# Reciprocal sums of attention: repeated along the row by VectorE and turned by two transposes, in place of four products with the identity

## The chip, the core and the metric

The kernel runs on one core of one Trainium2 chip. The metric is the device time of one execution in microseconds. In the profile, PE is TensorE's matrix multiplication and PEld its weight load, DVE is VectorE, ACT is ScalarE, POOL is GpSimd, and SP issues most DMAs.

## What is computed

One inference layer of a decoder with two parallel groups of heads over 1024 prompt tokens and 32 sample tokens (8 sequences of 4 tokens, over a paged cache of 8192 past tokens). Group A is sparse attention: 8 query heads, 2 key/value heads, head dimension 64, over the keys that an indexer selects. Group B is retention. The change lies in group A's attention for the prompt:

```python
logits = jnp.einsum('bqngd,bqknd->bqngk', qg, kg) * (HEAD_DIM ** -0.5)
logits = jnp.where(sel_ok[:, :, None, None, :], logits + bias, -jnp.inf)
probs = jax.nn.softmax(logits, axis=-1)
o = jnp.einsum('bqngk,bqknd->bqngd', probs, vg)
...
ya = jax.nn.silu(ga) * oa.reshape(B, T, D_A)
```

The softmax's division by the row sum, and the gate, are what the changed lines apply to the attention's output.

## The kernel before

The kernel runs input projections, the indexer's scores and selection, retention, attention, and last the output projection with the gated embedding. The order of instructions on each engine is laid out by a planner that works on a simulated timeline from the program's order and its dependences; some places are forced by high priorities and "issue after" marks. The profile shows the order that came out, not the planner's costs.

Attention over the prompt is a loop over 8 blocks of 128 queries (`qb`) and, inside, over the 2 key/value heads (`kv`): sixteen passes, counted 1 to 16 in this text. A pass has n = (qb + 1) * 128 keys and 4 query heads, and does this:

- `near` (L1757, VectorE, 128 x 1024): the relative bias of the last 256 keys plus the mask. The tile has two buffers, so pass k + 2 takes that of pass k.
- For each of the 4 heads (index `i4`), products of queries and keys into a bank `sa` (L1770, L1771, TensorE); VectorE adds `mask` or `near`, writes `L` and keeps the least value `mn` (L1776); ScalarE takes the exponential in place and sums each row into a column of `sm` (L1780). `L` has four buffers for each `kv`, so pass k + 2 writes those of pass k.
- For each block of 128 keys (`kb`), four transposes of the probabilities into a bank `ptp` (L1791, TensorE), a copy to `pT` in SBUF (L1796 on ScalarE, every third, L1794, on VectorE), and products with the values into `ob` (L1799, TensorE). The products for the two head positions `o` each fill 64 of the 128 columns of the array and 64 partitions of the bank.
- The reciprocal `rs` of `sm` (L1802, VectorE), 128 queries by 4 heads. It stands with queries on the partitions, and `ob` has queries along its rows, so the values are turned and repeated: four products with the identity (L1806, TensorE), with one column of `rs` repeated 64 times as the weights, fill `rb`. An fp32 product of this kind is two passes in the profile.
- `gat`, the gate's values for the pass, is multiplied by `rb` (L1809, VectorE), and `ob` by that into `yaT` (L1810, VectorE).

`rb` and `ptp` take turns in the two banks of tag "t". Two generators are worked off in between: `last_norm` (norms of retention, L1733 and L1735) and `sample_attn` (attention of the sample tokens: gathers of cached keys and values by POOL at L1268, transposes `pkg` and `pkw`, products `ls` and `oS`, and VectorE's work around them). A gather waits for the ScalarE instruction that stood latest in the loop when it was issued (L1780 or L1796).

The heads' order in `sm` is column i4 = 2 * o + c2, with o the head's half of the partitions and c2 its half of the columns in `rb`, `ob` and `gat`:

```python
rs = ap_.tile([128, 4], F32, tag="rs", bufs=2, name="rs")
nc.vector.reciprocal(rs, sm)
rb = bank("rb", "t")
for i4 in range(4):
    o, c2 = i4 // 2, i4 % 2
    nc.tensor.matmul(rb[64 * o:64 * o + 64, c2 * 128:c2 * 128 + 128],
                     rs[:, i4:i4 + 1].to_broadcast([128, 64]), ident, start=True, stop=True)
```

## Time and profile before

| what | value |
|---|---|
| median of three runs | 984.95 us (984.34 to 986.95) |
| the profiled execution | 987.33 us |
| its span, first to last instruction | 985.5 us |
| mean granted TensorE clock | 0.983 |
| TensorE busy | 929.4 us (94%) |
| VectorE busy | 643.0 us (65%) |
| ScalarE busy | 447.4 us (45%) |
| `yaT`, first to last of sixteen | 588.9 to 748.4 us |

A matrix product's end is modelled, so a busy TensorE is not TensorE at its peak, and the gaps between its weight loads tell more. A row of the timeline gives the start, the duration, the engine, the line, what is written from what, and in brackets the idle time before it and what ended it; neighbours of one kind are merged and counted.

### The profile page before, as it was taken

The page shows a single profiled execution, that of the slowest core. Times are in us where ns is not written, and L with a number is a line of the kernel's source. Part 1 is how long each engine was busy: PE and PEld are TensorE (multiplying, and loading weights), DVE is VectorE, ACT ScalarE, POOL GpSimd, SP SyncE. Part 2 cuts the span into 40 slices and gives each one's busy share as a digit, 9 for nine tenths or more (in the row PEclk, how much of TensorE's full clock was granted, in tenths as well). Part 3 has the DMA queues.
Part 4 walks back from the last instruction along what each step waited for, and adds up shares of the span by engine and source line. Part 5 has one row for each costly group of instructions (what it writes and reads, how often), then busy time and mean ns, then how long its engine had stood idle before and what let it go on. Part 6 is the DMA issues. An engine that isn't in the chain of part 4 may idle for free.

```text
span 985.5 us, 18931 instructions
## 1 busy us (share of the span) xinstructions
PE 929.4 (94%) x6980; PEld 786.5 (80%) x6980; DVE 643.0 (65%) x1917; ACT 447.4 (45%) x1001; POOL 324.4 (33%) x443
## 2 busy tenths in 40 slices
PE   4999996799998999999999988999999999999998
PEld 3888994467768988899889965666567999899998
DVE  6847668779954769979886467876654224954332
ACT  5645545346232876434333345565555334432210
POOL 4205125113405514516335036554314422133300
PEclk8999999899999999999999969999999999999999
DMA  8313233576544110341225365333222322522211
GB/s 267 119 68 110 102 97 96 199 240 216 173 149 122 44 45 7 82 97 45 61 72 124 102 182 170 108 110 99 60 67 64 107 65 75 165 74 87 93 35 38
DMA packets 102127, 104.36 MB, mean 106 GB/s; under 512 B 22002, under 2 KB 92210, under 8 KB 99602
## 3 DMA queue, kind: packets, MB, share of 16 engines
q1 hardware_dynamic: 96274, 76.93, 26.5%
q0 software_dynamic: 5760, 26.22, 8.7%
q8 instruction: 55, 0.90, 0.4%
q14 instruction: 38, 0.31, 0.1%
HBM read 80.36 MB, written 22.76 MB: 105 GB/s over the span
## 4 chain that ended last, share of the span: by engine, by line
PE 75%; DMA 9%; DVE 7%; issue 3%; ACT 2%; POOL 2%; SPq 2%; ACTq 0%; DVEq 0%; POOLq 0%
PE pb L277 5%; PE pb L278 4%; PE pb L279 4%; PE ob L1799 4%; PE ptp L1791 4%; PE pg L287 3%; PE pg L289 3%; PE pg L288 3%; PE po L287 3%; PE po L289 3%; PE po L288 3%; PE pvg L287 2%; PE pvg L288 2%; PE pvg L289 2%; PE pqk L287 2%
## 5 line engine op out<-in xcount | busy, mean ns | idle before, releaser
L1268 POOL DMA_INDIRECT kvs<-in_cache_kv,idx x64 | 63.3, 989 | 85.4 <-ACT pT L1796 33.8
L287 PE MATMUL pqk<-whi_qkb,xh 128*128 128x256 f32 x256 | 73.4, 287 | 2.7 <-DVE rp L1109 1.2
L287 PE MATMUL pvg<-whi_vgb,xh 128*128 128x256 f32 x256 | 75.1, 293 | 0.6 <-DVE rp L1109 0.6
L288 PE MATMUL pvg<-wlo_vgb,xh 128*128 128x256 f32 x256 | 73.7, 288 | 0.8 <-POOL wlo_vgb L197 0.8
L287 PE MATMUL po<-whi_o,yTh 128*128 128x256 f32 x256 | 73.3, 286 | 0.4 <-DVE yaT L1810 0.4
L288 PE MATMUL pqk<-wlo_qkb,xh 128*128 128x256 f32 x256 | 73.5, 287 | 0.0
L289 PE MATMUL pvg<-whi_vgb,xl 128*128 128x256 f32 x256 | 73.3, 286 | 0.0
L289 PE MATMUL po<-whi_o,yTl 128*128 128x256 f32 x256 | 72.9, 285 | 0.0
L289 PE MATMUL pqk<-whi_qkb,xl 128*128 128x256 f32 x256 | 72.8, 284 | 0.0
L287 PE MATMUL pg<-whi_g,yTh 128*128 128x256 f32 x256 | 72.7, 284 | 0.0
L288 PE MATMUL po<-wlo_o,yTh 128*128 128x256 f32 x256 | 72.6, 284 | 0.0
L289 PE MATMUL pg<-whi_g,yTl 128*128 128x256 f32 x256 | 72.3, 283 | 0.0
L288 PE MATMUL pg<-wlo_g,yTh 128*128 128x256 f32 x256 | 72.2, 282 | 0.0
L197 POOL TENSOR_TENSOR wlo_g<-wraw_g,whi_g 128x256 fp32r<-128x256 f32 x32 | 27.2, 881 | 88.1 <-ACT whi_g L196 88.0
L1780 ACT ACTIVATE L<-L,mn 128x128 f32<-128x128 f32 (+7 forms) x64 | 49.6, 777 | 13.2 <-DVE mn L1776 10.7
L1988 DVE TENSOR_TENSOR sgm<-pu,sgm 128x256 f32<-128x256 f32 x32 | 13.6, 424 | 64.2 <-PE pu L289 60.7
L545 DVE SCALAR_TENSOR_TENSOR score<-r,wi,score 128x384 f32<-128x384 f32 (+5 forms) x42 | 43.0, 1023 | 18.8 <-ACT r L544 16.7
L287 PEld LDWEIGHTS pqk<-whi_qkb,xh 128*128 128x128 f32 x256 | 48.3, 188 | 4.3 <-issue 2.3
L287 PEld LDWEIGHTS po<-whi_o,yTh 128*128 128x128 f32 x256 | 49.0, 191 | 2.2 <-issue 1.6
L287 PEld LDWEIGHTS pvg<-whi_vgb,xh 128*128 128x128 f32 x256 | 48.4, 189 | 2.7 <-PE pvg L296 0.8
L287 PEld LDWEIGHTS pg<-whi_g,yTh 128*128 128x128 f32 x256 | 48.8, 190 | 1.6 <-issue 1.2
L544 ACT ACTIVATE r<-si 128x384 f32<-128x384 f32 (+5 forms) x48 | 35.8, 758 | 30.2 <-PE si L386 20.7
(540 smaller groups left out, 3067.8 us busy)
## 6 DMA issues: line engine op xcount, KB each, us to landing
wraw_qkb<-in_w_in SPq DMA_DIRECT2D x16, 256.0 KB
wraw_vgb<-in_w_in SPq DMA_DIRECT2D x16, 256.0 KB
wraw_o<-in_w_out SPq DMA_DIRECT2D x8, 512.0 KB
qas<-qas_d SPq DMA_DIRECT2D x8, 512.0 KB
xr<-in_x_prompt SPq DMA_DIRECT2D x8, 512.0 KB
wraw_g<-in_w_ple_gate SPq DMA_DIRECT2D x8, 512.0 KB
out_y_prompt<-sgm SPq DMA_DIRECT2D x32, 128.0 KB
qas_d<-qst SPq DMA_DIRECT2D x8, 384.0 KB
```

Of the source, the lines that this page charges most:

```text
L277: nc.tensor.matmul(pt[:m, :n], wh, xh[:, k, ts], start=(k == 0), stop=False)
L278: nc.tensor.matmul(pt[:m, :n], wh, xl[:, k, ts], start=False, stop=False)
L279: nc.tensor.matmul(pt[:m, :n], wl, xh[:, k, ts], start=False, stop=(k == KC - 1))
L287: nc.tensor.matmul(pt[:, :n], ah, hi[:, k, :n], start=(k == 0), stop=False)
L288: nc.tensor.matmul(pt[:, :n], ah, lo[:, k, :n], start=False, stop=False)
L289: nc.tensor.matmul(pt[:, :n], al, hi[:, k, :n], start=False, stop=(k == kc - 1))
L544: nc.scalar.activation(r[:, :n], s[:, :n], AF.Relu)
L545: nc.vector.scalar_tensor_tensor(sc, r[:, :n], wi[:, qb, h:h + 1], sc if h else place[:, :n], op0=ALU.mult, op1=ALU.add)
L1268: return nc.gpsimd.indirect_dma_start(out=dst, out_offset=None, in_=kvflat, in_offset=bass.IndirectOffsetOnAxis(ap=idx, axis=0))
L1780: behind[0] = nc.scalar.activation(L[:, :n], L[:, :n], AF.Exp, bias=least, scale=-1.0, accum_out=sm[:, i4:i4 + 1])
L1791: nc.tensor.transpose(tp[:, i4 * 128:i4 * 128 + 128], P[i4][:, kb * 128:kb * 128 + 128], ident)
L1799: nc.tensor.matmul(ob[64 * o:64 * o + 64, :256], vtok[:, kb, kv * 64:kv * 64 + 64], pT[:, o * 256:o * 256 + 256], start=(kb == 0), stop=(k ...
```

## The change

The tile `rs` is gone; its name now stands for the first quarter of this pass's `near` (128 x 256), which has been read by then. VectorE's reciprocal reads each of the four values 64 times and writes 256, ordered so that a transpose of 128 columns puts each head's value on the 64 partitions of its half. Two full transposes on TensorE fill `rb`. What follows, `gat` and `yaT`, is as it was.

```diff
-            rs = ap_.tile([128, 4], F32, tag="rs", bufs=2, name="rs")
-            nc.vector.reciprocal(rs, sm)
+            rs = near[:, 0].rearrange("p (c x) -> p c x", c=2)
+            nc.vector.reciprocal(rs.rearrange("p c (o d) -> p c o d", o=2),
+                                 sm.rearrange("p (o c) -> p c o", o=2)[:, :, :, None].to_broadcast([128, 2, 2, 64]))
             rb = bank("rb", "t")
-            for i4 in range(4):
-                o, c2 = i4 // 2, i4 % 2
-                nc.tensor.matmul(rb[64 * o:64 * o + 64, c2 * 128:c2 * 128 + 128],
-                                 rs[:, i4:i4 + 1].to_broadcast([128, 64]), ident, start=True, stop=True)
+            for c2 in range(2):
+                nc.tensor.transpose(rb[:, c2 * 128:c2 * 128 + 128], rs[:, c2], ident)
```

Of the kernel before, what the change touches and what calls it, by code (L numbers as in the profile page):

```python
# [11 lines left out]
F32 = mybir.dt.float32  # L12
# [119 lines left out]
def tile_step(ctx: ExitStack, tc: tile.TileContext, I, O):  # L132
    nc = tc.nc

    def pool(name, bufs=1, **kw):
        return tc.tile_pool(name=name, bufs=bufs, reuse_waits="tile", **kw)
# [18 lines left out]
    def bank(name, tag="b"):  # L155
        if tag in kept.get("tags", ()):
            return kept["pool"].tile([128, 512], F32, tag="s", bufs=1, name=name)
        return psum["pool"].tile([128, 512], F32, tag=tag, bufs=psum["bufs"][tag], name=name)
# [6 lines left out]
    def C(name, rows=128):  # L165
        o, w = _CW[name]
        return cst[:rows, o:o + w]

    ident = C("ident")
# [342 lines left out]
    with pool("ix", side="right") as ix:  # L512
# [125 lines left out]
        def more():  # L638
            pace[0] += 0.3
            while pace[0] >= 1:  # L640
                pace[0] -= 1
                next(last, None)
# [178 lines left out]
    def step(gen, n=1):  # L821
        for _ in range(n):
            next(gen, None)
# [301 lines left out]
    def chunk_mm(qk, vv, tb, rows, mask_ap, hp):  # L1125

        r = bank("ret", "c")
        nc.tensor.transpose(r[:, 0:rows], qk[:rows, 0:128], ident[:rows, :rows])
        nc.tensor.transpose(r[:, 128:128 + rows], qk[:rows, 128:256], ident[:rows, :rows])
        qkT = rt.tile([128, 256], F32, tag="qkT", bufs=2, name="qkT")  # L1130
        rv = r[:, :256].rearrange("p (a r) -> p a r", a=2)[:, :, :rows]
        qv = qkT.rearrange("p (a r) -> p a r", a=2)[:, :, :rows]
        nc.scalar.copy(qv, rv)
        e = second[:, (tb % 4) * 128:(tb % 4) * 128 + 128]
        sm = rt.tile([128, 2, 128], F32, tag="sm", bufs=2, name="sm")
        for j, sc in enumerate((r[:rows, 256:256 + rows], e[:rows, :rows])):
            js = slice(j * 64, j * 64 + 64)
            nc.tensor.matmul(sc, qkT[js, 128:128 + rows], qkT[js, 0:rows], start=True, stop=True)
            nc.vector.tensor_tensor(sm[:rows, j, :rows], sc, mask_ap, op=ALU.mult)
        return r, qkT, sm  # L1140
# [452 lines left out]
    for hp in range(4):  # L1593
# [27 lines left out]
        for tb in range(8):  # L1621
# [8 lines left out]
            r, qkT, sm = chunk_mm(qk, vv, tb, 128, tri, hp)  # L1630
            o = r[:, 0:128]
# [10 lines left out]
            for j in range(2):  # L1642
                nc.tensor.matmul(o[:, j * 64:j * 64 + 64], sm[:, j, :], vv[:, j * 64:j * 64 + 64],
                                 start=(tb == 0 and j == 0), stop=(j == 1))
# [46 lines left out]
    ap_ = as_.enter_context(pool("att", side="right"))  # L1691
# [6 lines left out]
    def load_q(qb):  # L1698
        q = ap_.tile([128, 8, 128], F32R, tag="qas", bufs=2, name=f"qas{qb}")
        last_q[0] = nc.sync.dma_start(q.bitcast(F32), qas_d[:, :, qb * 128:(qb + 1) * 128]).ins  # L1700
        return q
# [41 lines left out]
    for qb in range(8):  # L1743
        qas = qnext
        if qb < 7:
            qnext = load_q(qb + 1)
            if qb == 3:
                with tc.issue_after(last_q[0]):
                    nc.sync.dma_start(gpost, I["g_post"].to_broadcast([128, D]))
        n = (qb + 1) * 128  # L1750
        w = min(n, 256)
        gat = ap_.tile([128, 4, 128], F32, tag="gat", bufs=2, name="gat")
        nc.sync.dma_start(gat, ga_d[:, :, qb * 128:n])
        mn_src = caus[:, 256 - w:] if qb < 2 else mask[:, OFF[qb] + n - w:OFF[qb] + n]
        for kv in range(2):
            near = ap_.tile([128, 4, 256], F32, tag="near", bufs=2, name="near")
            nc.vector.tensor_tensor(near[:, :, 256 - w:], toep[:, 4 * kv:4 * kv + 4, 256 - w:],  # L1757
                                    mn_src[:, None, :].to_broadcast([128, 4, w]), op=ALU.add)
            sm = ap_.tile([128, 4], F32, tag="sm", bufs=2, name="sm")
            P = []  # L1760
            for i4 in range(4):
                h = 4 * kv + 2 * (i4 % 2) + i4 // 2
                L = (atl, at)[kv].tile([128, T], F32, tag="L", bufs=4, name="L")
                P.append(L)
                mn = ap_.tile([128, 4], F32, tag="mn", bufs=4, name="mn")
                least, i = 3.0e38, 0
                for c in range(0, n, 512):
                    wc = min(512, n - c)
                    s = bank("sa")
                    nc.tensor.matmul(s[:, :wc], qas[:, h, :], kah[kv][:, c:c + wc], start=True, stop=False)  # L1770
                    nc.tensor.matmul(s[:, :wc], qas[:, h, :], kal[kv][:, c:c + wc], start=False, stop=True)  # L1771
                    cut = min(max(n - w, c), c + wc)
                    for x0, x1, add in ((c, cut, mask[:, OFF.get(qb, 0) + c:OFF.get(qb, 0) + cut]),
                                        (cut, c + wc, near[:, h - 4 * kv, cut - n + 256:c + wc - n + 256])):
                        if x1 > x0:
                            latest[0] = nc.vector.tensor_tensor_reduce(  # L1776
                                L[:, x0:x1], s[:, x0 - c:x1 - c], add, 1.0, least,
                                op0=ALU.add, op1=ALU.min, accum_out=mn[:, i:i + 1]).ins
                            least, i = mn[:, i:i + 1], i + 1
                behind[0] = nc.scalar.activation(L[:, :n], L[:, :n], AF.Exp, bias=least, scale=-1.0,  # L1780
                                                 accum_out=sm[:, i4:i4 + 1])
                more(0.4 + n / 1200)
            if qb > 1:
                step(ln)
            ob = bank("ob", "o")
            for kb in range(qb + 1):
                if kb == 1 and qb > 1:
                    step(ln)
                tp = bank("ptp", "t")
                for i4 in range(4):  # L1790
                    nc.tensor.transpose(tp[:, i4 * 128:i4 * 128 + 128], P[i4][:, kb * 128:kb * 128 + 128], ident)  # L1791
                pT = ap_.tile([128, 512], F32, tag="pT", bufs=4, name="pT")
                if kb % 3 == 2:
                    nc.vector.tensor_copy(pT, tp)  # L1794
                else:
                    behind[0] = nc.scalar.copy(pT, tp)  # L1796
                more(0.65)
                for o in range(2):
                    nc.tensor.matmul(ob[64 * o:64 * o + 64, :256], vtok[:, kb, kv * 64:kv * 64 + 64],  # L1799
                                     pT[:, o * 256:o * 256 + 256], start=(kb == 0), stop=(kb == qb))  # L1800
            rs = ap_.tile([128, 4], F32, tag="rs", bufs=2, name="rs")
            nc.vector.reciprocal(rs, sm)  # L1802
            rb = bank("rb", "t")
            for i4 in range(4):
                o, c2 = i4 // 2, i4 % 2
                nc.tensor.matmul(rb[64 * o:64 * o + 64, c2 * 128:c2 * 128 + 128],  # L1806
                                 rs[:, i4:i4 + 1].to_broadcast([128, 64]), ident, start=True, stop=True)
            gv = gat[:, 2 * kv:2 * kv + 2, :]
            nc.vector.tensor_tensor(gv, rb[:, :256].rearrange("p (c q) -> p c q", c=2), gv, op=ALU.mult)  # L1809
            nc.vector.tensor_tensor(yaT[:, 2 * kv:2 * kv + 2, qb * 128:n],  # L1810
                                    ob[:, :256].rearrange("p (c q) -> p c q", c=2), gv, op=ALU.mult)
            if qb > 1:
                step(ln)
# [219 lines left out]
```

## The prediction

> **What bounds the kernel now.** I read the page's totals first, then the stage of the change (attention, 580 to 750 us of the span) by engine, then the chain that ended last inside it, and last the single rows around the changed lines.
>
> The page, part 1:
>
> ```profile
> PE 929.4 (94%) x6980; PEld 786.5 (80%) x6980; DVE 643.0 (65%) x1917; ACT 447.4 (45%) x1001; POOL 324.4 (33%) x443
> ```
>
> The stage in four stretches:
>
> ```profile
> core 0: us, PE busy (x) PEld busy (x) DVE busy (x) ACT busy (x) POOL busy (x), PEclk, DMA share, GB/s
> 580.00:600.00 20.00, 16.91 (x100) 11.74 (x101) 14.80 (x60) 12.45 (x41) 10.70 (x10) 0.75 0.39 108
> 600.00:640.00 40.00, 37.73 (x296) 24.48 (x294) 34.16 (x137) 22.84 (x59) 22.51 (x24) 1.00 0.51 146
> 640.00:720.00 80.00, 80.00 (x599) 50.18 (x595) 56.10 (x199) 44.28 (x90) 35.41 (x37) 1.00 0.32 89
> 720.00:750.00 30.00, 28.92 (x239) 18.11 (x237) 13.68 (x48) 15.24 (x30) 4.04 (x4) 1.00 0.13 41
> ```
>
> The chain that ended last, cut to 580 to 750 us (437 pieces; its shares by line and its longest piece):
>
> ```profile
> by line: PE ob L1799 23.4%; PE ptp L1791 22.6%; PE sa L1770 11.8%; PE sa L1771 10.0%; PE oS L1533 4.9%; PE ls L1499 4.9%; PE rb L1806 4.4%; PE pkg L1485 3.9%; issue 2.4%; DMA kvs<-in_cache_kv,idx 2.1%; ACT L L1780 1.8%; ACT pT L1796 1.3%; P
> 599.15 3.55 DMA kvs<-in_cache_kv,idx
> ```
>
> TensorE holds the chain almost throughout, and the products with the identity (rb, L1806) are 4.4% of these 170 us, 7.5 us, or 0.47 us each. So work taken off TensorE here counts. But VectorE is not idle company: it is busy 74% of the first 20 us, 85% of the next 40, 70% of the next 80. There is one large hole on TensorE, 3.55 us at 599 us for a gather.
>
> **VectorE: one value becomes 256.** Before, the reciprocal takes 4 values per partition; after, the same 4 are read 64 times each and 256 quotients are written. The kernel has no reciprocal of that width, so its price comes from the narrow ones (three groups by line with their shapes, and the answers for three single lines, with least/median/greatest ns and first and last start):
>
> ```profile
> L1802 DVE RECIPROCAL rs<-sm x16: 158/172/180, 584.6 to 728.4; 128x4 f32<-128x4 f32 x16
> L260 DVE RECIPROCAL ry_x<-ry_x 128x1 f32<-128x1 f32 x8 | 1.2, 154 | 0.3 <-ACT ry_x L259 0.3
> L731 DVE RECIPROCAL wd<-wd 128x6 f32<-128x6 f32 x6 | 1.1, 182 | 0.2
> L1158 DVE RECIPROCAL gy<-gy 128x16 f32<-128x16 f32 x3 | 0.7, 235 | 0.0
> L1201 DVE RECIPROCAL wi<-wi x1: 266/266/266, 580.0 to 580.0; 128x18 f32<-128x18 f32 x1
> L1757 DVE TENSOR_TENSOR near<-toep,mask x12: 1205/1219/1361, 592.7 to 695.6; 128x1024 f32<-128x1024 f32 x12
> L1757 DVE TENSOR_TENSOR near<-toep,cst x4: 684/958/1225, 570.6 to 585.8; 128x512 f32<-128x512 f32 x2, 128x1024 f32<-128x1024 f32 x2
> ```
>
> From 4 to 16 values the time goes from 172 to 235 ns: 5.25 ns a value. From 1 to 6 it is (182 - 154)/5 = 5.6, from 4 to 18 it is (266 - 172)/14 = 6.7. Ordinary work is far cheaper: from 512 to 1024 elements L1757 goes from 684 to 1219 ns, 1.04 ns an element. So a reciprocal is not a streaming operation here, and 252 further values cost 252 x 5.25 = 1.32 us; the new instruction takes about 1.5 us. Bounds: 252 x 1.04 = 0.26 us more if wide ones stream, 252 x 6.7 = 1.69 us more by the steepest pair. I take 1.32, since all pairs of reciprocals lie at 5 to 7. Sixteen of them: +21.1 us (bounds 4.2 and 27.0).
>
> [...]
>
> What of the 21.1 us lies on the path? The reciprocals start at 584.6 to 728.4 us: four in the first stretch, five in the second, six in the third, one in the last. In 580 to 640 us VectorE is idle for 60 - 48.96 = 11.04 us, and nine reciprocals add 9 x 1.32 = 11.9: even if every gap could be used it does not fit. The gaps are waits for products of other engines, so I take half of them as usable: 11.9 - 5.5 = 6.4 us on the path (bounds: 0.9 with all usable, 11.9 with none). In 640 to 720 us 23.9 us idle stand against 6 x 1.32 = 7.9; I take 0.2 us for each, a late copy of pT (every third is VectorE's) or a late L: 1.2 us (bounds 0 and 7.9). The last one at 728 us has free time behind it: 0, its cover being TensorE's work until the end of attention; without it 1.3. Together +7.6.
>
> **TensorE: eight passes become two.** The rows of its weight loads at three places, in order of time, show what a change of column width costs, which no group shows:
>
> ```profile
> 590.27 0.19 PEld L1771 LDWEIGHTS sa<-kalo,qas 128*128 128x128 f32 x1
> 590.59 0.42 PEld L1806 LDWEIGHTS rb<-cst,rs 128*64 128x64 f32 x8
> 591.19 0.19 PEld L1770 LDWEIGHTS sa<-kahi,qas 128*128 128x128 f32 x1 [0.17 <-issue]
> ...
> 672.76 0.20 PEld L1799 LDWEIGHTS ob<-pT,vtok 128*64 128x64 f32 x4 [0.37 <-issue]
> 673.34 0.42 PEld L1791 LDWEIGHTS ptp<-cst,L 128*128 128x128 f32 x4 [0.39 <-issue]
> 673.93 0.20 PEld L1799 LDWEIGHTS ob<-pT,vtok 128*64 128x64 f32 x4 [0.17 <-issue]
> 674.20 0.63 PEld L1806 LDWEIGHTS rb<-cst,rs 128*64 128x64 f32 x8
> 675.00 0.42 PEld L1485 LDWEIGHTS pkg<-cst,kvs 128*128 128x128 f32 x4 [0.17 <-issue]
> ...
> 718.05 0.20 PEld L1799 LDWEIGHTS ob<-pT,vtok 128*64 128x64 f32 x4
> 718.32 0.63 PEld L1806 LDWEIGHTS rb<-cst,rs 128*64 128x64 f32 x8
> 718.87 0.30 PEld L1799 LDWEIGHTS ob<-pT,vtok 128*64 128x64 f32 x4
> ...
> 721.36 0.87 PEld L1791 LDWEIGHTS ptp<-cst,L 128*128 128x128 f32 x8
> ```
>
> Eight transposes load in 0.87 us, four in 0.42: 0.11 us each, so two add 0.22. Going from 64 columns (128*64, ob and rb) to 128 leaves the loader idle 0.39 us "for nothing the profile shows", going back 0.17. The old products stand in ob's width, the new transposes in ptp's. I count the sixteen places as they stand now:
> - three between full-width products (as at 590.59): rb takes 591.19 - 590.59 = 0.60, two transposes 0.22; saves 0.38 x 3 = 1.14.
> - seven behind ob and ahead of full width (as at 674.20): from ob to the next full-width load 675.00 - 673.93 = 1.07; without rb it is 673.34 - 672.76 = 0.58, with two transposes 0.80; saves 0.27 x 7 = 1.89.
> - four between two ob (as at 718.32): now 718.87 - 718.05 = 0.82; from ob over four transposes to ob it is 673.93 - 672.76 = 1.17, over two 0.95; loses 0.13 x 4 = 0.52.
> - two between ob and 32-column products; about 0.1 each saved by the same differences, 0.2.
>
> That is 2.7 us saved. If all sixteen fell beside full-width work it would be 16 x 0.38 = 6.1; if all fell between two ob, a loss of 2.1. I take 2.7, since the order around them is not the change's. In all 128 passes become 32 (two for a product, as x8 for four shows; one for a transpose, as x4 for a bank of ptp shows), and their issue is inside these differences.
>
> [...]
>
> **The tile rs becomes the first quarter of near.** Nothing is saved or spent on memory that shows, but near has two buffers, so the one for the pass after next may now be written only when this pass's transposes have read it; before, it waited only for the L that add it. Two passes early and two late, VectorE's and TensorE's rows (near of passes 3 and 16; the reciprocal of pass 14 and rb of passes 1 and 14), and what frees L in pass 14 (released by the ptp just ahead of rb of pass 12):
>
> ```profile
> 582.69 1.23 DVE L1757 TENSOR_TENSOR near<-toep,cst 128x1024 f32<-128x1024 f32 x1
> 585.90 1.13 PE L1806 MATMUL rb<-cst,rs 128*64 128x128 f32 x8
> ...
> 695.57 1.23 DVE L1757 TENSOR_TENSOR near<-toep,mask 128x1024 f32<-128x1024 f32 x1
> 696.74 0.18 DVE L1802 RECIPROCAL rs<-sm 128x4 f32<-128x4 f32 x1
> 718.54 0.66 PE L1806 MATMUL rb<-cst,rs 128*64 128x128 f32 x8
> ...
> 686.22 0.69 DVE L1776 CUSTOM_DVE_ANT_0 L<-sa,mask 128x512 f32<-128x512 f32 x1 [2.51 <-PE ptp L1791]
> 686.71 0.63 PEld L1806 LDWEIGHTS rb<-cst,rs 128*64 128x64 f32 x8
> ```
>
> Near runs 3 us (early) to 23 us (late) ahead of the transposes that it will have to wait for, in all fourteen cases. So it will move, from VectorE's free time to just behind rb. Its reader hardly comes earlier: the four L of a pass are freed by the last ptp of the pass two before, half a us ahead of rb there. In late passes the mask part of L comes first and covers the wait; behind near in VectorE's queue stand then the copies of pT and the L parts, for which ACT's exponentials wait. In passes 3 and 4 near is needed at once; the hole of 3.55 us for the gather stands behind them as cover, and without it they cost 2 x 1.22 us. Bounds: 0, and 14 x 1.22 = 17.1 us if all came on the path. I take 0, as the free place is half a us from where L starts anyway.
>
> DMAs, ScalarE's work, SP's queue and POOL's gathers do not change in number. The gathers wait for ACT's copies of pT, so they shift with them.
>
> **Sum.** +7.6 (VectorE) - 2.7 (TensorE) + 0 (near) = +4.9 us. The profiled execution took 987.33 us with a span of 985.5, 2.4 above the median of the three runs: 992.2 by it, 989.9 by the median 984.95. I say 990.
>
> **Rivals.**
> - VectorE's extra is hidden (faster). If the planner puts each reciprocal where VectorE waits anyway, or wide reciprocals stream (0.26 us), only TensorE's saving is left: 2.7 to 6.1 us, 979 to 982. For it: between 640 and 720 us nearly three times the idle time that is needed, and products that come 21.8 us after their reciprocal in pass 14 (696.74 and 718.54). Against: 11.9 us into 11.0 in 580 to 640. It decides once less than 2.7 us of the 21.1 stay on the path.
> - The two cancel: 2 to 5 us of VectorE on the path, 985 plus or minus 3.
> - Near's wait is the bound: the fourteen come on the path with 17.1 us, less 2.7: +14.4, 999. For it: near moves in every pass, and 600 to 640 us has VectorE at 85%. Against: L is freed next to it.
> - VectorE's value costs more than the slope that I took: at 6.7 ns nine instructions add 15.2 us in 580 to 640, 9.7 of it beyond half the gaps, with 1.2 and -2.7: +8.2, 993; with every extra on the path (27.0 - 2.7) 1009. [...]
>
> **How the numbers follow.** Forecast (+3 to +9, 988 to 994): 0.42. Hidden: 0.18. Cancelled: 0.22. Near: 0.08. Dearer value or more of it on the path: 0.10. A measurement of this kernel tells about 0.3%, 3 us, from no change. Faster 0.18, same 0.24 (0.22 and the forecast's lower edge), slower 0.58. The range leaves out the best case's end and the worst: 981 to 1001.
>
> **What would show it.** The stage is read from the first to the last yaT:
>
> ```profile
> L1810 DVE TENSOR_TENSOR yaT<-ob,gat x16: 394/420/426, 588.9 to 748.4; 128x256 f32<-128x256 f32 x16
> ```
>
> Its length, 588.9 to 748.4 us, should grow by about 5 us, and the rest stay unchanged. Further: the reciprocal at L1801 to L1803 at 1.3 to 1.8 us x16 and VectorE's total up by about 21 us; rb with 32 instead of 128 passes; near starting after the transposes of the pass two before, with an idle ahead of it or moved in order; VectorE above 90% in the 60 us from the start of attention. Wrong if the reciprocal streams, if the chain of the stage is as solid on TensorE as before, or if the order of work changes elsewhere.

## The result

| kernel | median | runs | ratio, 95% interval |
|---|---|---|---|
| before | 984.64 us | 4 (983.35 to 986.95) | |
| after | 998.03 us | 4 (995.92 to 998.7) | 1.0128 (1.0102 to 1.0155) |

The change costs 1.28%, 12.6 us. The direction is as forecast, the size is not: +5 was said, and the value lies in the upper part of the range. The profiled execution of the changed kernel took 998.04 us, 10.7 more than that of before. Later comparisons are each made against runs of the kernel before on the same chip, whose median went from 984.5 to 989.6 us with the chip; so the ratios are what to compare.

The changed kernel's page, its totals, and the four stretches of the stage, as shown for the kernel before:

```profile
PE 934.3 (94%) x6884; PEld 786.6 (79%) x6884; DVE 665.1 (67%) x1917; ACT 449.3 (45%) x1001; POOL 323.5 (32%) x443
```

```profile
580.00:600.00 20.00, 15.63 (x72) 11.28 (x72) 15.18 (x50) 10.85 (x37) 9.13 (x8) 0.59 0.32 94
600.00:640.00 40.00, 34.29 (x236) 21.01 (x233) 34.95 (x116) 20.46 (x54) 18.91 (x20) 0.96 0.46 137
640.00:720.00 80.00, 75.68 (x536) 47.38 (x535) 66.02 (x204) 43.34 (x91) 33.60 (x37) 0.98 0.31 87
720.00:750.00 30.00, 29.70 (x206) 17.67 (x203) 21.05 (x62) 18.60 (x34) 7.86 (x9) 1.00 0.23 68
```

VectorE's total rises by 22.1 us, TensorE executes 96 passes fewer. Yet TensorE is less busy in the first three stretches, with holes that it did not have, while VectorE goes from 70 to 83% in the third. The chain that ended last in the stage (580 to 750 us), and the one wait of TensorE that grew most, of before and after (580 to 745 us; total us, times, longest):

```profile
by line: PE ob L1799 17.3%; PE ptp L1791 16.5%; DMA kvs<-in_cache_kv,idx 11.0%; PE sa L1770 8.6%; PE sa L1771 6.9%; issue 4.7%; PE ls L1499 4.2%; DVE L L1776 4.2%; PE oS L1533 3.3%; ACT L L1780 3.2%; PE pkg L1485 2.7%; ACT pT L1796 1.6%; PE
```

```profile
PEld pkg L1485 <- DMA kvs<-in_cache_kv,idx: 1.2, 1, 1.2
```

```profile
PEld pkg L1485 <- DMA kvs<-in_cache_kv,idx: 8.0, 7, 1.9
```

The gathers of cached keys hold 11% of the chain, 2.1% before. That looks like a cause; an experiment below takes this wait away, and the loss stays. The changed instructions:

```profile
L1802 DVE RECIPROCAL near<-sm x16: 1730/1746/1753, 585.0 to 743.9; 128x256 f32<-128x256 f32 x16
L1806 PEld LDWEIGHTS rb<-cst,near x32: 137/142/230, 586.8 to 758.4; 128*128 128x128 f32 x32
L1757 DVE TENSOR_TENSOR near<-toep,mask x12: 1162/1212/1218, 601.1 to 731.6; 128x1024 f32<-128x1024 f32 x12
L1809 DVE TENSOR_TENSOR yaT<-ob,gat x16: 358/416/425, 590.7 to 759.7; 128x256 f32<-128x256 f32 x16
```

The reciprocal takes 1.746 us, sixteen of them 25.2 us more than before. The last near starts at 731.6 us, before at 695.6: it has moved behind the transposes. From the first to the last yaT it is 169.0 us, before 159.5. How one reciprocal stands in VectorE's queue, in the timeline (the transposes of pass 10, then near and the L of pass 12, with pass 11's reciprocal among them):

```profile
675.20 0.20 PEld L1806 LDWEIGHTS rb<-cst,near 128*128 128x128 f32 x2 [0.38 <-issue]
...
676.02 1.22 DVE L1757 TENSOR_TENSOR near<-toep,mask 128x1024 f32<-128x1024 f32 x1
676.06 0.28 PE L1771 MATMUL sa<-kalo,qas 128*128 128x256 f32 x1
...
677.76 0.69 DVE L1776 CUSTOM_DVE_ANT_0 L<-sa,mask 128x512 f32<-128x512 f32 x1
678.38 1.75 DVE L1802 RECIPROCAL near<-sm 128x256 f32<-128x256 f32 x1
...
678.70 0.28 PE L1771 MATMUL sa<-kalo,qas 128*128 128x256 f32 x1
...
680.32 0.47 DVE L1776 CUSTOM_DVE_ANT_0 L<-sa,near,mn 128x256 f32<-128x256 f32 x1
...
680.40 0.14 PEld L1485 LDWEIGHTS pkg<-cst,kvs 128*128 128x128 f32 x1 [1.39 <-DMA kvs<-in_cache_kv,idx]
...
680.72 0.48 DVE L1776 CUSTOM_DVE_ANT_0 L<-sa,near,mn 128x256 f32<-128x256 f32 x1
```

The two L with near, at 680.32 and 680.72, read banks that the products at 676.06 and 678.70 had filled, at 676.34 and 678.98; both stood behind the reciprocal in VectorE's order. Meanwhile TensorE, in its own order, stood 1.39 us at keys that had not landed.

### The profile page after: what moved, and what is told of

It reads as the page before. It is cut to its first block, busy times and chain, and to the rows that moved or that the text cites. A ratio compares the mean times of both kernels' runs of the same rounds, so it can differ in the third digit from the quotient of the medians.

```text
span 996.2 us, 18764 instructions
## 1 busy us (share of the span) xinstructions
PE 934.3 (94%) x6884; PEld 786.6 (79%) x6884; DVE 665.1 (67%) x1917; ACT 449.3 (45%) x1001; POOL 323.5 (32%) x443
## 4 chain that ended last, share of the span: by engine, by line
PE 71%; DVE 10%; DMA 9%; issue 4%; ACT 3%; POOL 2%; SPq 1%; DVEq 0%; ACTq 0%; POOLq 0%
PE pb L277 5%; PE pb L278 4%; PE pb L279 4%; PE ob L1799 3%; PE pg L287 3%; PE ptp L1791 3%; PE pg L289 3%; PE pg L288 3%; PE po L287 3%; PE po L288 3%; PE po L289 3%; PE pvg L287 2%; PE pvg L288 2%; PE pvg L289 2%; PE pox L879 2%
## 5 line engine op out<-in xcount | busy, mean ns | idle before, releaser
L1268 POOL DMA_INDIRECT kvs<-in_cache_kv,idx x64 | 65.4, 1022 | 97.0 <-ACT pT L1796 38.3
L1780 ACT ACTIVATE L<-L,mn 128x128 f32<-128x128 f32 (+7 forms) x64 | 49.4, 774 | 12.8 <-DVE mn L1776 12.5
L1791 PE MATMUL ptp<-cst,L 128*128 128x128 f32 x288 | 50.9, 295 | 1.7 <-ACT L L1780 1.2
L1791 PEld LDWEIGHTS ptp<-cst,L 128*128 128x128 f32 x288 | 32.8, 145 | 24.1 <-issue 18.3
```

The source lines that it names most:

```text
L1268: return nc.gpsimd.indirect_dma_start(out=dst, out_offset=None, in_=kvflat, in_offset=bass.IndirectOffsetOnAxis(ap=idx, axis=0))
L1780: behind[0] = nc.scalar.activation(L[:, :n], L[:, :n], AF.Exp, bias=least, scale=-1.0, accum_out=sm[:, i4:i4 + 1])
L1791: nc.tensor.transpose(tp[:, i4 * 128:i4 * 128 + 128], P[i4][:, kb * 128:kb * 128 + 128], ident)
```

## The experiments

Four theories were tested. V: the long reciprocal's time on VectorE is the loss. N: near's wait for the transposes is. P: any edit makes the planner lay out another order, and the loss is a draw of that. G: the loss goes by way of the gathers.

| kernel | ratio to before, 95% | at 985 us |
|---|---|---|
| changed | 1.0128 (1.0102 to 1.0155) | +12.6 |
| changed, storage of its own for the 256 values | 1.0129 (1.0090 to 1.0167) | +12.7 |
| long reciprocal alone, products as before | 1.0153 (1.0123 to 1.0182) | +15.1 |
| half as long, products as before | 1.0055 (1.0032 to 1.0079) | +5.4 |
| long one added, read by nobody | 1.0117 (1.0088 to 1.0145) | +11.5 |
| short reciprocal, VectorE copy, near waits | 1.0045 (1.0019 to 1.0071) | +4.4 |
| the same, near free | 0.9988 (0.9964 to 1.0011) | -1.2 |
| near's wait alone, first runs | 1.0043 (1.0017 to 1.0070) | +4.2 |
| near's wait alone, second runs | 1.0029 (1.0014 to 1.0045) | +2.9 |
| changed, reciprocal in four pieces, near free | 1.0085 (1.0056 to 1.0114) | +8.4 |
| changed, reciprocal held back | 1.0148 (1.0111 to 1.0184) | +14.6 |

**Storage of its own.** The 256 values go to two stretches of the constants that the attention no longer needs.

```diff
-            rs = near[:, 0].rearrange("p (c x) -> p c x", c=2)
+            rs = C(("cos", "sin")[kv])[:, :256].rearrange("p (c x) -> p c x", c=2)
```

> The whole change, but the 256 repeated reciprocals lie in storage of their own (a stretch of the constants that is no longer read), so near is free as early as before. Theory V (VectorE's longer reciprocal, 1.75 us in place of 0.17, is the loss): 994 to 999 us, as the changed kernel. Theory N (near, taken up two passes on, waits for the transposes): back to 982 to 987. Theory P (the planner lays out another order, in which TensorE meets cached keys that have not landed; each edit gives a draw of its own): anywhere from 984 to 999, and the more idle time of TensorE ends with the gathered keys, the slower.

+1.29%, the changed kernel's loss. Taking near's wait away brings nothing back; N falls as the cause of this loss.

**The long reciprocal alone.** As above, and the products with the identity as before.

```diff
-            for c2 in range(2):
-                nc.tensor.transpose(rb[:, c2 * 128:c2 * 128 + 128], rs[:, c2], ident)
+            for i4 in range(4):
+                o, c2 = i4 // 2, i4 % 2
+                nc.tensor.matmul(rb[64 * o:64 * o + 64, c2 * 128:c2 * 128 + 128],
+                                 rs[:, c2, 64 * o:64 * o + 64], ident, start=True, stop=True)
```

> VectorE's part alone: 256 repeated reciprocals in storage of their own, and the four products with the identity as before (their weights are 64 repeated columns instead of one column read 64 times). V: 996 to 1001, the changed kernel without TensorE's saving of about 3 us. N: 984 to 988. P: anywhere from 985 to 1000.

+1.53%: V holds. With the run above, on the same chip, it also prices TensorE's part: 1000.08 with products, 996.83 with transposes, 3.2 us less, though the two intervals overlap.

**Half the length.** Before with 128 values, each of the four 32 times.

```diff
-            rs = ap_.tile([128, 4], F32, tag="rs", bufs=2, name="rs")
-            nc.vector.reciprocal(rs, sm)
+            rs = C(("cos", "sin")[kv])[:, :128].rearrange("p (c o d) -> p c o d", c=2, o=2)
+            nc.vector.reciprocal(rs, sm.rearrange("p (o c) -> p c o", o=2)[:, :, :, None].to_broadcast([128, 2, 2, 32]))
...
-                                 rs[:, i4:i4 + 1].to_broadcast([128, 64]), ident, start=True, stop=True)
+                                 rs[:, c2, o, 0:1].to_broadcast([128, 64]), ident, start=True, stop=True)
```

> The kernel before with a reciprocal of 128 values (each of the 4 repeated 32 times) in storage of its own; the four products read one column each as before. At the 6.25 ns a value that the changed kernel shows it should take 0.95 us, 0.78 more than before, 12.4 us in sixteen passes: half of what the 256 values add. If each added us of VectorE costs its share (proportional): +7.5 us, 992. If the free time of VectorE takes up the first half and only the rest costs: +2 to +4, 986 to 989. If any other laying-out of the order costs alike, whatever VectorE's load: +12 to +15.

+5.4 us for 12.4 us of VectorE, between the two forecasts: the first half costs 0.44 of its time, and from here to the long one (+9.7 for 12.8 us) 0.76. The interval, 3.2 to 7.8 us, holds the proportional +7.5 too, so that the second half costs more is not shown. The price of a value, from the groups by line of this kernel, of the long one alone and of the pieces below:

```profile
L1802 DVE RECIPROCAL cst<-sm 128x128 f32<-128x128 f32 x16 | 15.1, 946 | 1.6 <-ACT L L1780 1.6
```

```profile
L1802 DVE RECIPROCAL cst<-sm 128x256 f32<-128x256 f32 x16 | 27.9, 1744 | 2.9 <-ACT L L1780 2.9
```

```profile
L1784 DVE RECIPROCAL cst<-sm 128x64 f32<-128x64 f32 x64 | 34.7, 544 | 5.6 <-ACT L L1780 4.8 <-issue 0.8
```

From 64 to 128 values 6.28 ns each, from 128 to 256 6.23.

**A load without a consumer.** Before, with a long reciprocal behind the short one, written where nobody reads it.

```diff
             nc.vector.reciprocal(rs, sm)
+            nc.vector.reciprocal(C(("cos", "sin")[kv])[:, :256].rearrange("p (a d) -> p a d", a=4),
+                                 sm[:, :, None].to_broadcast([128, 4, 64]))
```

> The kernel before, with a reciprocal of 256 values added behind the narrow one, whose result nobody reads: VectorE's time alone, 16 x 1.75 = 28 us, with no consumer. If the loss is VectorE's occupation (other work stands behind the long instruction): +13 to +18, 998 to 1003 beside 985. If the loss is that the products or transposes wait for a longer reciprocal: within 3 us of before.

+1.17%, a little below what V expected: it is VectorE's occupation that costs, not a product that waits longer for its reciprocal.

**A short reciprocal and a copy**, once into near (near waits), once into storage of its own.

```diff
+            r4 = ap_.tile([128, 4], F32, tag="rs", bufs=2, name="rs")
+            nc.vector.reciprocal(r4, sm)
             rs = near[:, 0].rearrange("p (c x) -> p c x", c=2)
-            nc.vector.reciprocal(rs.rearrange("p c (o d) -> p c o d", o=2),
-                                 sm.rearrange("p (o c) -> p c o", o=2)[:, :, :, None].to_broadcast([128, 2, 2, 64]))
+            nc.vector.tensor_copy(rs.rearrange("p c (o d) -> p c o d", o=2),
+                                  r4.rearrange("p (o c) -> p c o", o=2)[:, :, :, None].to_broadcast([128, 2, 2, 64]))
```

> The change with a narrow reciprocal (4 values) and a VectorE copy that repeats them into near's first quarter; transposes and near's wait stay. The copy should take 0.3 to 0.45 us, so VectorE is relieved of some 18 us of the added 25. V: 984 to 988. N: 995 to 999, as the changed kernel. P: anywhere from 984 to 999.

> Narrow reciprocal (4 values), a VectorE copy of 0.29 us that repeats them into storage of their own, two transposes: no longer reciprocal, and near does not wait. If near's wait is worth the 4 us that the run with this wait alone showed: 983 to 986. If the 4.4 us of the run with copy and near came from the copy's 4.6 us on VectorE instead: 988 to 990. With nothing but TensorE's saving: 982.

+0.45% with near's wait, -0.12% without: repeating by a copy takes back all that the long reciprocal costs, and then near's wait shows, some 0.57% (5.6 us) between the two. The copy, in the second kernel:

```profile
L1804 DVE COPY cst<-rs x16: 278/291/480, 592.6 to 739.2; 128x256 f32<-128x256 f32 x16
```

0.29 us for what costs 1.57 us by reciprocals. The two transposes' saving is not to be told from nothing here (interval 0.9964 to 1.0011).

**Near's wait alone**, in the kernel before; run twice.

```diff
-            rs = ap_.tile([128, 4], F32, tag="rs", bufs=2, name="rs")
+            rs = near[:, 0, :4]
             nc.vector.reciprocal(rs, sm)
```

> The kernel before with only one thing changed: the 4 reciprocals are written into near's first four columns, and the four products read them there, so near waits as in the changed kernel. V: 984 to 986. N: 994 to 999. P: not the same as before although nothing was added, 982 to 996.

> The kernel before with near's wait alone, once more and in more rounds: its first runs gave +0.43% but the one profile put less than 1 us into attention, its start having been 7 us late. If near's wait costs time by itself: +4 to +6, with attention longer by as much in the profile. If the first result was the scatter of what comes ahead of attention: within 2 us of before.

+0.43% and +0.29%, so by itself it does cost 3 to 4 us. First near, fourth and last yaT of the first kernel's execution, then of the second's, and the fourth yaT of before:

```profile
577.64 1.29 DVE L1757 TENSOR_TENSOR near<-toep,cst 128x512 f32<-128x512 f32 x2 [0.76 <-DMA toep<-toep_d]
...
610.55 0.42 DVE L1810 TENSOR_TENSOR yaT<-ob,gat 128x256 f32<-128x256 f32 x1
...
756.12 0.42 DVE L1810 TENSOR_TENSOR yaT<-ob,gat 128x256 f32<-128x256 f32 x1 [2.62 <-PE ob L1799]
```

```profile
L1757 DVE TENSOR_TENSOR near<-toep,cst x4: 684/954/1218, 573.7 to 594.8; 128x512 f32<-128x512 f32 x2, 128x1024 f32<-128x1024 f32 x2
...
610.34 0.42 DVE L1810 TENSOR_TENSOR yaT<-ob,gat 128x256 f32<-128x256 f32 x1
...
756.24 0.42 DVE L1810 TENSOR_TENSOR yaT<-ob,gat 128x256 f32<-128x256 f32 x1 [2.61 <-PE ob L1799]
```

```profile
607.36 0.42 DVE L1810 TENSOR_TENSOR yaT<-ob,gat 128x256 f32<-128x256 f32 x1
```

Attention starts 3.9 us apart and ends 0.1 us apart; before it starts at 570.6. So these two executions of one kernel reached attention 3.9 us apart, and at the fourth yaT 0.2 us of that is left. Behind the fourth pass the two agree: 145.6 and 145.9 us to the last yaT, where before takes 141.0 and the three kernels with a copy and near free 139.8 to 141.0. So the wait's cost lies there in both traces; with a copy and near's wait it is less clear (141.9).

**Without the gathers' wait**, in both kernels.

```diff
-                    if behind[0] is not None:
-                        tc.add_manual_dep(got.ins, behind[0].ins.name, mybir.DependencyInfo(
-                            mybir.DependencyClass.Sync, mybir.DependencyReason.DATA))
```

> The changed kernel, but the gathers of cached keys and values no longer wait for ScalarE's latest exponential or copy (a pacing wait; what they need of data and buffers they still wait for). Theory G (VectorE's longer reciprocal makes ScalarE's pieces later, the gathers wait for these, and TensorE, in order, stands at the transposes of keys that have not landed): most of the loss goes by this wait, so this kernel against the same edit of the kernel before is at most 5 us slower, and TensorE's idle time ended by gathered keys falls from 8 us to about 1. Theory V (VectorE's throughput itself is the bound): still 10 to 14 us slower than the same edit of the kernel before.

> The kernel before without the gathers' wait for ScalarE: the control of the run above. The gathers start earlier and meet other transfers; 980 to 992, by itself nothing that tells the theories apart.

1049.55 and 1036.86 us, 1.0611 and 1.0473 times before. The difference stays at 12.7 us, as V said, and in neither trace does TensorE wait for gathered keys any more. But with both kernels some 50 us slower this alone does not decide.

**Nobody waits for the gathered keys**, in both kernels (toep is noted in keys where it is made). The sample tokens' attention reads toep in place of what was gathered.

```diff
-            kw = kws[p % 2]
-            kv = [kvs[(2 * p + j) % 4] for j in range(2)]
+            kw = keys[0][:, :2]
+            kv = [keys[0], keys[0]]
```

> The kernel before, but the sample tokens' attention reads its cached keys and values from the table of biases, which lies in SBUF and has the shape, instead of from what was gathered; the gathers run as before and nobody waits for them (this leaves the sample outputs' use of the cache out). Control of the next run. TensorE stood 1.2 us at gathered keys before, so 982 to 986.

> The changed kernel with the same edit: TensorE never waits for gathered keys. Theory G (the longer reciprocal costs time by way of the gathers: ScalarE's pieces late, gathers late, TensorE in order stands at keys that have not landed, 8 us in the changed kernel's profile): the difference to the control falls from 12.6 to 5 us or less. Theory V (VectorE's throughput and the queue behind each reciprocal): still 10 to 13 us over the control, with the idle time now ended by ScalarE's copies, L and banks.

985.80 and 999.13 us: 13.3 us apart by the medians, 15.3 by the two ratios (1.0122 / 0.9968 = 1.0155). G falls. Who waits instead, in the waits of the first and the second (580 to 760 us):

```profile
ACT L L1781 <- DVE mn L1777: 13.1, 15, 3.0
```

```profile
ACT L L1781 <- DVE mn L1777: 33.0, 20, 3.8
```

ScalarE's exponentials stand 20 us longer for VectorE's least values. The same wait in before and in the changed kernel themselves:

```profile
ACT L L1780 <- DVE mn L1776: 10.7, 14, 1.8
```

```profile
ACT L L1780 <- DVE mn L1776: 12.5, 19, 2.0
```

There it hardly grows, and TensorE's wait for keys grows by 6.8 us. That this is the same lateness, seen where TensorE's next instruction happened to be the gathers', is a reading and not shown. In the six other kernels with more values to take, those on the gathers aside, the wait is 15.6 to 22.0 us; in the eight executions with the short reciprocal alone it is 9.0 to 14.7 (580 to 765 us).

**In four pieces.** 64 values behind each head's exponential, in storage of their own.

```diff
+                o, c2 = i4 // 2, i4 % 2
+                rs = C(("cos", "sin")[kv])[:, :256].rearrange("p (c x) -> p c x", c=2)
+                nc.vector.reciprocal(rs[:, c2, 64 * o:64 * o + 64], sm[:, i4:i4 + 1].to_broadcast([128, 64]))
```

> The change with the reciprocals split: 64 values behind each head's exponential, into storage of their own, four instructions of about 0.55 us in place of one of 1.75 us; 2.2 us a pass, so 7 us more of VectorE in all. Throughput (VectorE's sum in the stage counts): +15 to +20 over before. Blocking (L, mn and copies stand behind one long instruction, short ones let them through): +3 to +9.

+0.85% with 34.7 us of reciprocals in place of 27.9 (the rows above). By VectorE's sum alone it should be slower than the undivided one. It is rather faster, but the intervals (0.56 to 1.14 and 0.90 to 1.67%) overlap: short blocks may soften it, and that is not settled.

**Held back** until the pass's last copy of pT (turned_ names it) has been issued.

```diff
+            with tc.issue_after(turned_.ins):
+                nc.vector.reciprocal(rs.rearrange("p c (o d) -> p c o d", o=2),
```

> The changed kernel with the long reciprocal held back until the pass's last copy of the turned probabilities has been issued, in place of as soon as the sums are there. Throughput: +11 to +14, as the changed kernel. Blocking of the L parts and exponentials two passes on: +4 to +8, as it then stands where a pass ends. If its product is then waited for by TensorE: over +14.

+1.48% (1.11 to 1.84%), more than the +4 to +8 us of blocking: another place does not help. Between the other two forecasts it does not decide.

**The copy on other engines**, with a short reciprocal and near free.

> Narrow reciprocal, the repeating copy by ScalarE into storage of its own, two transposes. VectorE's work is that of the kernel before, TensorE saves about 2.5 us, ScalarE (55% busy in the stage) gets 16 copies of about 0.35 us: 980 to 985 if ScalarE's copies are hidden, 985 to 989 if they delay exponentials and copies.

> The same with GpSimd making the repeating copy, about 1 us each behind the gathers in its queue, which wait for ScalarE: 981 to 985 if the products come late enough, 986 to 995 if the copies stand behind waiting gathers and the banks of the transposes are held.

1.0006 (0.9985 to 1.0026) with ScalarE's copy, 1.0000 (0.9981 to 1.0019) with GpSimd's; the copies take 0.40 us on each, where about 1 us was expected of GpSimd:

```profile
L1804 ACT COPY cst<-rs x16: 387/404/428, 588.0 to 730.4; 128x256 f32<-128x256 f32 x16
```

```profile
L1804 POOL COPY cst<-rs x16: 396/403/1114, 584.4 to 727.4; 128x256 f32<-128x256 f32 x16
```

Neither beats the kernel before. P is not borne out as the cause: the kernels with 256 reciprocals a pass lose 0.85 to 1.53%, the three with a copy and near free lie within 0.12% of before, although each has an order of its own. The profiled executions say the same, from the first near to the last yaT: 177.8 us before, 176.7 to 179.4 in those three, 184.2 with 128 values, 185.8 to 194.4 in the six with 256.

## Why the prediction was wrong in size

- **A value's price.** The slope taken from 4 to 18 values was right in kind, and the rival of a streaming reciprocal is gone. Its size was low: 5.25 ns was said, 6.2 to 6.3 are measured, close to the steepest pair of rows (6.7). That is 25.2 us in place of 21.1. With the share unchanged it makes 9.1 us on the path and a sum of +6.4: the price alone explains 1.5 us of the miss.
- **The share on the path: this step failed.** 7.6 of 21.1 us were put on the path, 0.36; the long reciprocal alone shows 15.1 of 25.2, 0.60, the load without a consumer 11.5 of 27.5, 0.42 (their intervals overlap). Within it the stretch from 640 us was taken for nearly free, 1.2 us. The eighth and the last yaT of before, of the changed kernel, and of the long reciprocal alone:

```profile
640.39 0.42 DVE L1810 TENSOR_TENSOR yaT<-ob,gat 128x256 f32<-128x256 f32 x1 [0.19 <-PE ob L1799]
...
748.37 0.42 DVE L1810 TENSOR_TENSOR yaT<-ob,gat 128x256 f32<-128x256 f32 x1 [2.61 <-PE ob L1799]
```

```profile
648.87 0.42 DVE L1809 TENSOR_TENSOR yaT<-ob,gat 128x256 f32<-128x256 f32 x1
...
759.69 0.42 DVE L1809 TENSOR_TENSOR yaT<-ob,gat 128x256 f32<-128x256 f32 x1 [0.46 <-PE oT L1539]
```

```profile
644.10 0.42 DVE L1811 TENSOR_TENSOR yaT<-ob,gat 128x256 f32<-128x256 f32 x1
...
757.36 0.42 DVE L1811 TENSOR_TENSOR yaT<-ob,gat 128x256 f32<-128x256 f32 x1
```

  The changed kernel is 8.5 us late by pass 8, 1.0 of it from ahead of the first near; 6.4 was said for about this part. By the last pass it is 11.3 late, 2.8 more in spite of TensorE's saving. The long reciprocal alone is 3.7 and then 9.0 late: 5.3 us more where 1.2 was said. From pass 8 to the last it is 108.0 us before and 106.6 to 109.9 in the three kernels with a copy and near free, 110.8 in the changed kernel, 113.3 to 114.4 with the long reciprocal alone, with storage of its own and with the load. These are single executions; that of the long reciprocal alone was the fastest of its four.

  The idle VectorE was taken for room, and the trace of before did have room: behind the reciprocals of passes 13 and 14 VectorE stood idle for 2.51 us (the prediction shows the row at 686.22) and 2.13 us. Before, and the same two passes in the changed kernel:

```profile
683.55 0.16 DVE L1802 RECIPROCAL rs<-sm 128x4 f32<-128x4 f32 x1
...
699.05 0.58 DVE L1505 CUSTOM_DVE_ANT_0 pr<-ls,MA 64x416 f32<-64x416 f32 x1 [2.13 <-PE ls L1499]
```

```profile
701.05 1.74 DVE L1802 RECIPROCAL near<-sm 128x256 f32<-128x256 f32 x1
702.71 0.24 DVE L1776 CUSTOM_DVE_ANT_0 L<-sa,mask,mn 128x128 f32<-128x128 f32 x1
...
715.37 1.75 DVE L1802 RECIPROCAL near<-sm 128x256 f32<-128x256 f32 x1
717.03 0.36 DVE L1809 TENSOR_TENSOR yaT<-ob,gat 128x256 f32<-128x256 f32 x1
```

  There the next instruction follows at once. The gaps belonged to the old order, and in the new one work stands behind the reciprocal. Nor was VectorE above 90% from 580 to 640 us, as was expected: it is busy 84%, before 82%. Its free time there was not filled, the work took longer. Which way the lateness of L and of the exponentials reaches TensorE in the changed kernel is not shown step by step.
- **TensorE's saving.** 2.7 us were said; 3.2 us is the difference between the two long-reciprocal kernels, within their scatter. The idle time between column widths (the 0.39 us rows) stays: the transposes at 675.20 us in the timeline above stand behind ob with 0.38 us idle. What it is due to no run shows.
- **Near's wait.** It was put at 0, and in this change nothing of it is seen (1.0128 with it, 1.0129 without), though these two intervals would hide some 4 us. The reason given was wrong: without the long reciprocal it costs 3 to 6 us. That the long reciprocal covers it is likely, not shown. The other bound, 17.1 us, is far off.
- **The cover by the gather's hole** did not stay as it was: TensorE's idle time for gathers grew from 1.2 to 8.0 us, without being the cause. The 3.55 us of the prediction were the transfer's own time in the chain; TensorE stood 1.2 us for it.
- **The rest unchanged.** From the last yaT to the end it is 996.2 - 759.7 = 236.5 us, before 237.1.

The result lies at the rival of the dearer value with more of it on the path, 0.10 of the chance, in place of the forecast.

## What to carry to other kernels

Here a reciprocal was paid by the value, 0.17 us for 4 and 1.75 us for 256, and a copy from 4 values to 256 took 0.29 us: so take it on the narrow tile and repeat the result with the copy. Free time of an engine that feeds the bound was slack here only in the order in which it was seen: the 2.51 and 2.13 us that VectorE idled behind two reciprocals of before were gone in the order that the new instruction gave. A load of the planned length that nobody reads, put into the kernel before, prices it first: here +11.5 us. And where an engine, in its order, idles at some transfer, take that wait away before calling it the cause: here the whole loss stayed (13.3 us without it, 12.6 with it).

## What was not expected of the hardware

- A reciprocal of fp32 cost 6.2 to 6.3 ns a value from 64 to 256 values here (0.54, 0.95, 1.75 us), against 0.29 us for a copy that writes 256 values from 4.
- Letting the gathers go without their wait for ScalarE slowed the kernel by 4.7%; the changed one came to 6.1% over before, in place of 1.3%. Why was not tried.
